# Feed-forward layers of a two-layer decoder trunk emitted as one planned stream

## The chip, the cores and the metric

One core of a Trainium2 chip runs the whole forward pass. The metric is the device time of one execution, in microseconds (us). The kernel before takes 2194.31 us, the median of three runs (2193.89 to 2194.33). Engines are named as in the profile: PE is TensorE's matmul, PEld its weight load, ACT is ScalarE, DVE is VectorE, POOL is GpSimd, SP is SyncE, which here only issues DMAs.

## The reference

The input x is 256 tokens by 2048 channels, float32. Each of two layers normalises, applies a mixer, adds the result to x, normalises again, applies the feed-forward part, and adds again. The mixer of layer 0 is a chunkwise matrix-memory recurrence beside a spatial-gating network, that of layer 1 is attention on keys chosen by an indexer. The change hardly touches the mixers. The feed-forward part is the same in both layers:

```
def conv_ffn(xn, w_up, conv_w, conv_b, w_down):      # 2048 -> 2*5632 -> 2048
    h = xn @ w_up
    h = depthwise_causal_conv(h, conv_w, width=3) + conv_b
    a, b = jnp.split(h, 2, axis=-1)
    return (jax.nn.silu(a) * b) @ w_down
```

All of it is wanted in float32 accuracy.

## The kernel before

**Matmuls in three passes.** Every operand is split into two halves that TensorE multiplies fast: hi, the value rounded to the type fp32r, and lo, what is left. A product is hi*hi + lo*hi + hi*lo: `mm3` (L175) issues three matmuls, L177, L178 and L179. The activations are the stationary operand, 128 tokens at a time, and the weights the moving one, 512 columns at a time. So a k-tile of 128 rows takes three matmuls for each of the two token halves.

**Loads and casts.** `load_w` (L88) brings one block of weights, four k-tiles by 512 columns, 1 MB, into a `raw` buffer with one DMA on SP (L93). Then it makes hi on ACT (a copy) and lo on DVE (raw minus hi), two k-tiles in one instruction; both are recorded under L65, the line of a helper. There are four `raw` buffers, four `hi` and four `lo` buffers, so hi and lo hold two blocks and raw four.

**Feed-forward.** `ffn` (L858) works in two parts, of 24 and of 20 tiles of 128 hidden channels. In a part it goes through the up-projection in groups of 512 columns, first four tiles of a, then the matching four of b, and so on; then it runs the down-projection of that part. A group is 16 k-tiles, four blocks, accumulated in two PSUM tiles `mm` (one per token half). The last block of a group is ordered so that the first token half ends first. There are 22 groups in a layer.

**What follows a group.** `up_job` (L819) is a Python generator that is resumed once per block by `pump` (L78). First it scales the PSUM tiles by the norm's factor on ACT (L823) and transposes 32x32 squares on DVE (L824) into `turn`. `LAG` blocks later 16 DMAs of 32 KB (L833) put the squares in place in a tile `A`, so that channels lie on partitions. Then the convolution runs for four tiles, two per resumption: ACT L840, DVE L842 and L844, and for the a half Silu on ACT (L847), for the b half the product with a (DVE L852) and the split into `yh` (ACT L184) and `yl` (DVE L185), which feed the down-projection.

**Order.** Code emits instructions in Python order, and a scheduler of the framework then orders each engine's queue, by the place of emission and by when buffers come free. Nothing fixes the order of casts against convolution on ACT and DVE. `resid` (L298) adds the down-projection to x in `h` and starts `norm_job` (L211), which transposes and splits the next layer's input; its end (L240 to L247) spreads the norm's factor over a row tile `rbc`, with four small matmuls in the profile (two instructions, L242). Only the mixer of layer 0 reads `rbc`, in `ch_sum`. `ch_proj` (L151), used twelve times in that mixer, has weights stationary and both activation halves side by side as the moving operand of 512 columns; a second matmul of 256 columns adds lo of the weights.

`out_steps(ktiles, row0, late)` (L316) lists the blocks of a down-projection. With `late` above zero the last `late` k-tiles of its first two column blocks come after the earlier ones of both.

## Time and profile before

| | |
|---|---|
| median of 3 runs | 2194.31 us |
| the profiled execution | 2193.54 us, span of the trace 2191.8 us |
| PE busy | 2168.8 us, 99% of the span |
| PEld busy | 1780.8 us, 81% |
| DVE busy | 1374.1 us, 63% |
| ACT busy | 1130.1 us, 52% |
| granted TensorE clock | 1.00 of full speed throughout |
| DMA | 425.51 MB, mean 194 GB/s |

The profile is one execution. The span runs from the first to the last instruction of the trace; the execution's own time is 1.7 us longer. Busy time is the time in which an engine has an instruction under way. Matmuls overlap one another, and their ends are modelled, so PE's busy share is not its speed. Each instruction has a start, a length, a line of the kernel, the tile it writes and those it reads, and, where the engine sat idle before it, what ended that wait.

### The profile page before, as it was taken

The page shows a single profiled execution, that of the slowest core. Times are in us where ns is not written, and L with a number is a line of the kernel's source. Part 1 is how long each engine was busy: PE and PEld are TensorE (multiplying, and loading weights), DVE is VectorE, ACT ScalarE, POOL GpSimd, SP SyncE. Part 2 cuts the span into 40 slices and gives each one's busy share as a digit, 9 for nine tenths or more (in the row PEclk, how much of TensorE's full clock was granted, in tenths as well). Part 3 has the DMA queues.
Part 4 walks back from the last instruction along what each step waited for, and adds up shares of the span by engine and source line. Part 5 has one row for each costly group of instructions (what it writes and reads, how often), then busy time and mean ns, then how long its engine had stood idle before and what let it go on. Part 6 is the DMA issues. An engine that isn't in the chain of part 4 may idle for free.

```text
span 2191.8 us, 27024 instructions
## 1 busy us (share of the span) xinstructions
PE 2168.8 (99%) x9948; PEld 1780.8 (81%) x9948; DVE 1374.1 (63%) x1903; ACT 1130.1 (52%) x1661; POOL 49.2 (2%) x69
## 2 busy tenths in 40 slices
PE   8999999999999999999999999999999999999999
PEld 7888888887778888777889888888777788877787
DVE  5455565575776446676656887556666754576664
ACT  6544555464555345555545566545555533554542
POOL 0011100000000000000000001000000000000000
PEclk9999999999999999999999999999999999999999
DMA  8555555667677556767656444456667655677673
GB/s 279 182 173 168 177 183 191 196 185 216 195 199 239 192 192 183 231 187 217 214 155 209 154 154 153 160 191 186 208 199 229 216 199 190 184 206 216 203 238 115
DMA packets 412033, 425.51 MB, mean 194 GB/s; under 512 B 198620, under 2 KB 236028, under 8 KB 411900
## 3 DMA queue, kind: packets, MB, share of 16 engines
q1 hardware_dynamic: 410476, 421.55, 62.0%
q10 hardware_dynamic: 1424, 2.23, 0.3%
q8 instruction: 78, 1.28, 0.3%
q14 instruction: 55, 0.45, 0.1%
HBM read 398.54 MB, written 2.10 MB: 183 GB/s over the span
## 4 chain that ended last, share of the span: by engine, by line
PE 78%; DVE 8%; issue 5%; ACT 4%; DMA 4%; POOL 0%; SPq 0%; ACTq 0%; DVEq 0%; POOLq 0%
PE mm L179 24%; PE mm L178 23%; PE mm L177 23%; PE mm L163 4%; DVE lo L65 3%; DMA raw<-in_ffn_w_up 3%; PE mm L161 2%; ACT hi L65 2%; ACT conv L840 2%; DVE conv L844 1%; DVE conv L842 1%; DVE turn L824 1%; DMA raw<-in_ffn_w_down 1%; PE tr L218 1%; DVE conv L852 1%
## 5 line engine op out<-in xcount | busy, mean ns | idle before, releaser
L65 DVE TENSOR_TENSOR lo<-raw,hi 128x1024 fp32r<-128x1024 f32 (+3 forms) x764 | 917.2, 1217 | 528.3 <-ACT hi L65 509.2
L65 ACT CAST hi<-raw 128x1024 fp32r<-128x1024 f32 (+3 forms) x764 | 779.0, 1037 | 629.3 <-PE mm L178 546.8
L177 PE MATMUL mm<-hi,xc 128*128 128x512 f32 (+3 forms) x1920 | 742.1, 387 | 9.3 <-ACT hi L65 8.7
L179 PE MATMUL mm<-lo,xc 128*128 128x512 f32 (+3 forms) x1920 | 737.8, 387 | 1.8
L178 PE MATMUL mm<-hi,xc 128*128 128x512 f32 (+3 forms) x1920 | 736.6, 384 | 0.0
L177 PEld LDWEIGHTS mm<-hi,xc 128*128 128x128 f32 x1920 | 360.9, 188 | 87.9 <-ACT hi L65 20.5
L179 PEld LDWEIGHTS mm<-lo,xc 128*128 128x128 f32 x1920 | 358.7, 188 | 85.4 <-DVE lo L65 19.4
L178 PEld LDWEIGHTS mm<-hi,xc 128*128 128x128 f32 x1920 | 361.1, 188 | 67.4
L177 PE MATMUL mm<-hi,yh 128*128 128x512 f32 x960 | 376.8, 394 | 1.7 <-ACT hi L65 1.6
L178 PE MATMUL mm<-hi,yl 128*128 128x512 f32 x960 | 375.8, 391 | 0.4 <-DVE yl L185 0.4
L179 PE MATMUL mm<-lo,yh 128*128 128x512 f32 x960 | 375.0, 392 | 0.3
L177 PEld LDWEIGHTS mm<-hi,yh 128*128 128x128 f32 x960 | 180.2, 188 | 42.1 <-ACT hi L65 3.3
L179 PEld LDWEIGHTS mm<-lo,yh 128*128 128x128 f32 x960 | 180.0, 188 | 41.5 <-DVE lo L65 2.9
L178 PEld LDWEIGHTS mm<-hi,yl 128*128 128x128 f32 x960 | 180.4, 188 | 39.2 <-DVE yl L185 1.2
L824 DVE STREAM_TRANSPOSE turn<-mm 128x512 f32<-128x512 f32 x88 | 62.8, 714 | 188.6 <-ACT mm L823 188.6
L823 ACT ACTIVATE mm<-mm,rstd 128x512 f32<-128x512 f32 x88 | 58.1, 660 | 210.7 <-PE mm L179 206.6
L163 PE MATMUL mm<-xc,hi 128*128 128x512 f32 x360 | 126.8, 395 | 0.0
L161 PE MATMUL mm<-xc,lo 128*128 128x256 f32 x384 | 106.2, 282 | 0.0
L840 ACT ACTIVATE conv<-A,conv 128x256 f32<-128x256 f32 x176 | 98.4, 594 | 1.3
L844 DVE SCALAR_TENSOR_TENSOR conv<-A,conv,conv 128x254 f32<-128x254 f32 x176 | 82.5, 480 | 3.5
L842 DVE SCALAR_TENSOR_TENSOR conv<-A,conv,conv 128x255 f32<-128x255 f32 x176 | 80.9, 472 | 4.8 <-ACT conv L840 4.8
L163 PEld LDWEIGHTS mm<-xc,hi 128*128 128x128 f32 x360 | 67.6, 188 | 15.1
(207 smaller groups left out, 861.0 us busy)
## 6 DMA issues: line engine op xcount, KB each, us to landing
raw<-in_ffn_w_up SPq DMA_DIRECT2D x176, 1024.0 KB
raw<-in_ffn_w_down SPq DMA_DIRECT2D x88, 1024.0 KB
raw<-in_even_w_in SPq DMA_DIRECT2D x44, 1024.0 KB
raw<-in_odd_w_in SPq DMA_DIRECT2D x24, 1024.0 KB
A<-turn SPq DMA_DIRECT2D x704, 32.0 KB
raw<-in_even_w_out SPq DMA_DIRECT2D x16, 1024.0 KB
raw<-in_odd_w_out SPq DMA_DIRECT2D x16, 1024.0 KB
raw<-in_odd_w_in SPq DMA_DIRECT2D x12, 736.0 KB
```

The lines of the kernel that those rows point to most:

```text
L65: ins = call(*args, **kw).ins
L161: nc.tensor.matmul(ps[ct][:, 1], wlo[:, c], x[:, 0], start=False, stop=False)
L163: nc.tensor.matmul(ps[ct], whi[:, c], x, start=False, stop=kt == KT - 1)
L177: nc.tensor.matmul(ps, ah, bh, start=start, stop=False)
L178: nc.tensor.matmul(ps, al, bh, start=False, stop=False)
L179: return nc.tensor.matmul(ps, ah, bl, start=False, stop=stop)
L218: nc.tensor.transpose(tp[:, tt * P:(tt + 1) * P], self.h[:, tt, kt * P:(kt + 1) * P], self.ident)
L823: nc.scalar.activation(ps[tt], ps[tt], AF.Copy, scale=self.rstd[:, tt:tt + 1])
L824: nc.vector.transpose(T[:, :, tt], ps[tt].rearrange("p (c t) -> p c t", c=4))
L840: nc.scalar.activation(y, A[:, ct], AF.Identity, bias=conv[:, 3, c:c + 1], scale=conv[:, 2, c:c + 1])
L842: nc.vector.scalar_tensor_tensor(y[:, 1:], A[:, ct, :S - 1], conv[:, 1, c:c + 1], y[:, 1:], op0=ALU.mult, op1=ALU.add)
L844: nc.vector.scalar_tensor_tensor(y[:, 2:], A[:, ct, :S - 2], conv[:, 0, c:c + 1], y[:, 2:], op0=ALU.mult, op1=ALU.add)
```

## The change

The two parts of a feed-forward layer, up and down, are put into one list of blocks, `plan`, and `stream` goes through it. At place i it emits the loads up to place i + 5 and the casts up to place i + 2, then the matmuls of place i; then it resumes the jobs and, at a group's end, starts the eviction. `flowed` chains every load, cast, eviction, transpose, turn DMA and convolution of the layer to the one emitted before it on the same engine, so that ACT, DVE and SP take them in the order of emission. `up_job` loses its lag and does one tile of convolution per block. The down-projection uses `late` = 4. `norm_job` stops after the norm's factor, except for the norm at the kernel's head. `ch_proj` issues hi for both column tiles, then lo for both, and lo is added to the other half of the PSUM tile. Buffers and their numbers stay as they are.

```diff
--- before.py
+++ after.py
@@ -31,7 +31,8 @@
 
 RAW = 2048
 HALF = 1024
-LAG = 3
+FETCH = 5
+CAST = 2
 
 NAMES = ["x", "mix_norm", "even_w_in", "even_i_bias", "even_f_bias", "even_a_norm",
          "even_b_norm", "even_spatial", "even_spatial_bias", "even_w_out", "odd_w_in",
@@ -145,6 +146,68 @@
                 evac(n, c0, ps)
                 del open_ps[n]
 
+    def flowed(self, eng, call, *args, **kw):
+        prev = self.flow.get(eng)
+        with self.tc.issue_after(prev) if prev is not None else nullcontext():
+            self.flow[eng] = call(*args, **kw).ins
+
+    def stream(self, plan):
+        nc = self.nc
+        raws, parts, open_ps, seen = [], [], {}, {}
+
+        def fetch(w, ktiles, step, lhs, evac, pre):
+            n, c0, ncol, k0, nk, row0 = step
+            raw = self.wraw.tile([P, RAW], F32, tag="raw", name="raw")
+            r0 = (row0 + k0) * P
+            self.flowed("p", nc.sync.dma_start, raw[:, :nk * ncol].rearrange("p (k c) -> p k c", k=nk),
+                        w[r0:r0 + nk * P, c0:c0 + ncol].rearrange("(k p) c -> p k c", p=P))
+            raws.append(raw)
+
+        def cast(w, ktiles, step, lhs, evac, pre):
+            n, c0, ncol, k0, nk, row0 = step
+            raw, per, got = raws[len(parts)], HALF // ncol, []
+            for s in range(0, nk, per):
+                m = min(per, nk - s)
+                hi = self.whi.tile([P, HALF], F32R, tag="hi", name="hi")
+                lo = self.wlo.tile([P, HALF], F32R, tag="lo", name="lo")
+                src, u = raw[:, s * ncol:(s + m) * ncol], m * ncol
+                self.flowed("s", nc.scalar.copy, hi[:, :u], src)
+                self.flowed("v", nc.vector.tensor_tensor, lo[:, :u], src, hi[:, :u], op=ALU.subtract)
+                got += [(k0 + s + i, hi[:, i * ncol:(i + 1) * ncol], lo[:, i * ncol:(i + 1) * ncol])
+                        for i in range(m)]
+            parts.append(got)
+
+        self.flow = {}
+        for i, (w, ktiles, step, lhs, evac, pre) in enumerate(plan):
+            if pre is not None:
+                pre()
+            n, c0, ncol, k0, nk, row0 = step
+            acts = [lhs(k0 + j) for j in range(nk)]
+            while len(raws) < min(i + 1 + FETCH, len(plan)):
+                fetch(*plan[len(raws)])
+            while len(parts) < min(i + 1 + CAST, len(plan)):
+                cast(*plan[len(parts)])
+            if n not in open_ps:
+                open_ps[n] = [self.mm.tile([P, 512], F32, tag="mm", name="mm") for _ in range(NT)]
+                seen[n] = 0
+            ps, work = open_ps[n], []
+            for (kt, whi, wlo), (ah, al) in zip(parts[i], acts):
+                work.append((ah, al, whi, wlo, seen[n] == 0, seen[n] == ktiles - 1))
+                seen[n] += 1
+            order = [(tt, j) for j in range(nk) for tt in range(NT)]
+            if seen[n] == ktiles:
+                order.sort()
+            for tt, j in order:
+                ah, al, whi, wlo, first, last = work[j]
+                t = slice(tt * P, (tt + 1) * P)
+                self.mm3(ps[tt][:, :ncol], ah[:, t], al[:, t], whi, wlo, first, last)
+            parts[i] = None
+            self.pump()
+            if seen[n] == ktiles:
+                evac(n, c0, ps)
+                del open_ps[n]
+        self.flow = None
+
     def tok_steps(self, n, c0, ncol, per=4, k0=0, k1=KT, row0=0):
         return [(n, c0, ncol, k, min(per, k1 - k), row0) for k in range(k0, k1, per)]
 
@@ -155,12 +218,10 @@
             for kt, whi, wlo in self.load_w(w, k0, 8, c0, 2 * P):
                 x = self.x_both(kt)
                 for ct in range(2):
-                    c = slice(ct * P, (ct + 1) * P)
-                    if kt == 0:
-                        nc.tensor.matmul(ps[ct], whi[:, c], x, start=True, stop=False)
-                    nc.tensor.matmul(ps[ct][:, 1], wlo[:, c], x[:, 0], start=False, stop=False)
-                    if kt > 0:
-                        nc.tensor.matmul(ps[ct], whi[:, c], x, start=False, stop=kt == KT - 1)
+                    nc.tensor.matmul(ps[ct], whi[:, ct * P:(ct + 1) * P], x, start=kt == 0, stop=False)
+                for ct in range(2):
+                    nc.tensor.matmul(ps[ct][:, 0], wlo[:, ct * P:(ct + 1) * P], x[:, 0],
+                                     start=False, stop=kt == KT - 1)
             self.pump()
         evac(ps)
 
@@ -235,6 +296,8 @@
         nc.vector.tensor_scalar(self.var, s, 1.0 / D, EPS, op0=ALU.mult, op1=ALU.add)
         self.rsqrt(self.rstd, self.var)
         self.ready.add("rstd")
+        if not head:
+            return
         yield 1
         yield 1
         tp = self.tr.tile([P, S], F32, tag="tr", name="tr")
@@ -820,40 +883,38 @@
         nc = self.nc
         T = fg.tile([P, 4, NT, P], F32, tag="turn", name="turn", bufs=2)
         for tt in range(NT):
-            nc.scalar.activation(ps[tt], ps[tt], AF.Copy, scale=self.rstd[:, tt:tt + 1])
-            nc.vector.transpose(T[:, :, tt], ps[tt].rearrange("p (c t) -> p c t", c=4))
-        yield 1
-        for _ in range(LAG):
-            yield 1
+            self.flowed("s", nc.scalar.activation, ps[tt], ps[tt], AF.Copy, scale=self.rstd[:, tt:tt + 1])
+            self.flowed("v", nc.vector.transpose, T[:, :, tt], ps[tt].rearrange("p (c t) -> p c t", c=4))
+        yield 1
         there = T.rearrange("p c t (q e) -> p q (c t) e", q=4)
         here = A.rearrange("p c (t i e) -> p i (c t) e", t=NT, i=4)
         for i in range(4):
             for q in range(4):
                 src, dst = slice(32 * i, 32 * i + 32), slice(32 * q, 32 * q + 32)
-                nc.sync.dma_start(here[dst, i], there[src, q])
+                self.flowed("p", nc.sync.dma_start, here[dst, i], there[src, q])
             if i % 2:
                 yield 1
         yield 1
         for ct in range(4):
             y = fg.tile([P, S], F32, tag="conv", name="conv")
             c = cc + ct
-            nc.scalar.activation(y, A[:, ct], AF.Identity, bias=conv[:, 3, c:c + 1],
-                                 scale=conv[:, 2, c:c + 1])
-            nc.vector.scalar_tensor_tensor(y[:, 1:], A[:, ct, :S - 1], conv[:, 1, c:c + 1], y[:, 1:],
-                                           op0=ALU.mult, op1=ALU.add)
-            nc.vector.scalar_tensor_tensor(y[:, 2:], A[:, ct, :S - 2], conv[:, 0, c:c + 1], y[:, 2:],
-                                           op0=ALU.mult, op1=ALU.add)
+            self.flowed("s", nc.scalar.activation, y, A[:, ct], AF.Identity, bias=conv[:, 3, c:c + 1],
+                        scale=conv[:, 2, c:c + 1])
+            for j in (1, 2):
+                self.flowed("v", nc.vector.scalar_tensor_tensor, y[:, j:], A[:, ct, :S - j],
+                            conv[:, 2 - j, c:c + 1], y[:, j:], op0=ALU.mult, op1=ALU.add)
             if sa is None:
-                nc.scalar.activation(A[:, ct], y, AF.Silu)
+                self.flowed("s", nc.scalar.activation, A[:, ct], y, AF.Silu)
                 self.ready.add(("a", c))
             else:
                 kt = kt0 + ct
                 assert ("a", c - 44) in self.ready
-                nc.vector.tensor_tensor(y, sa[:, ct], y, op=ALU.mult)
-                self.split(self.yh[kt // 4][:, kt % 4], self.yl[kt // 4][:, kt % 4], y)
+                self.flowed("v", nc.vector.tensor_tensor, y, sa[:, ct], y, op=ALU.mult)
+                hi, lo = self.yh[kt // 4][:, kt % 4], self.yl[kt // 4][:, kt % 4]
+                self.flowed("s", nc.scalar.copy, hi, y)
+                self.flowed("v", nc.vector.tensor_tensor, lo, y, hi, op=ALU.subtract)
                 self.ready.add(("y", kt))
-            if ct % 2:
-                yield 1
+            yield 1
 
     def ffn(self, l, gcol, final):
         nc, I, tc = self.nc, self.I, self.tc
@@ -862,30 +923,37 @@
         self.ready -= {("a", c) for c in range(44)}
         with tc.tile_pool(name=f"ff{l}", bufs=1) as ff, tc.tile_pool(name=f"fg{l}", bufs=2) as fg:
             As = [ff.tile([P, 4, S], F32, name=f"A{i}") for i in range(4)]
-
-            base = 0
+            plan, base = [], 0
             for part, nk in enumerate((24, 20)):
-                yh, yl = self.new_y(self.acts, 4)
-                eh, el = self.new_y(ff, (nk - 16) // 4, 4)
-                self.yh, self.yl = yh + eh, yl + el
+                last = part == 1
+
+                def open_y(nk=nk):
+                    yh, yl = self.new_y(self.acts, 4)
+                    eh, el = self.new_y(ff, (nk - 16) // 4, 4)
+                    self.yh, self.yl = yh + eh, yl + el
+
+                def up_evac(A, cc, sa, j):
+                    def evac(n, c0, ps):
+                        self.ensure("rstd")
+                        self.start(self.up_job(fg, ps, A, cc, conv, sa, j), now=True)
+                    return evac
+
+                pre = open_y
                 for j in range(0, nk, 4):
                     turn = (base + j) // 4 % 2
                     for half in range(2):
-                        A = As[2 * turn + half]
-                        sa = As[2 * turn] if half else None
-                        cc = 44 * half + base + j
-
-                        def evac(n, c0, ps):
-                            self.ensure("rstd")
-                            self.start(self.up_job(fg, ps, A, cc, conv, sa, j), now=True)
-
-                        self.tok_plan(w_up, self.x_at, KT, self.tok_steps(0, cc * P, 512), evac)
-                last = part == 1
-                if last and not final:
-                    self.new_xT()
-                self.tok_plan(w_down, self.y_at, nk, self.out_steps(nk, base, 0),
-                              self.resid(gcol if last else None, final=final and last))
+                        A, cc = As[2 * turn + half], 44 * half + base + j
+                        evac = up_evac(A, cc, As[2 * turn] if half else None, j)
+                        for step in self.tok_steps(0, cc * P, 512):
+                            plan.append((w_up, KT, step, self.x_at, evac, pre))
+                            pre = None
+                pre = self.new_xT if last and not final else None
+                evac = self.resid(gcol if last else None, final=final and last)
+                for step in self.out_steps(nk, base, 4):
+                    plan.append((w_down, nk, step, self.y_at, evac, pre))
+                    pre = None
                 base += nk
+            self.stream(plan)
 
     def run(self):
         self.new_xT()
```

On ACT, from the first eviction of the fifth group of layer 0 on, the order was (L823 is the eviction, L65 a cast, L840 the convolution's start, L184 makes yh):

```order
L823 ACTIVATE mm<-mm,rstd 128x512
L65 CAST hi<-raw 128x1024 x2
L823 ACTIVATE mm<-mm,rstd 128x512
L840 ACTIVATE conv<-A_3389,conv_101 128x256 x2
L184 CAST yh_3391<-conv 128x256 x2
L65 CAST hi<-raw 128x1024 x2
L840 ACTIVATE conv<-A_3389,conv_101 128x256 x2
L65 CAST hi<-raw 128x1024 x4
L184 CAST yh_3391<-conv 128x256 x2
```

and in the changed kernel (all under L152, the line in `flowed`), around the evictions of the third group:

```order
L152 CAST hi<-raw 128x1024 x2
L152 ACTIVATE conv<-A_3387,conv_101 128x256
L152 CAST yh_3390<-conv 128x256
L152 ACTIVATE mm<-mm,rstd 128x512 x2
L152 CAST hi<-raw 128x1024 x2
L152 ACTIVATE conv<-A_3387,conv_101 128x256
L152 CAST yh_3390<-conv 128x256
L152 CAST hi<-raw 128x1024 x2
L152 ACTIVATE conv<-A_3387,conv_101 128x256
L152 CAST yh_3390<-conv 128x256
```

Two tiles of convolution stood together between casts; now each pair of casts, one block's, is followed by one tile's convolution, and both evictions of a group stand together behind one of them.

On DVE, after the two transposes (L824) of the fourth group, all four tiles of a convolution (L842, L844) came before six casts:

```order
L824 STREAM_TRANSPOSE turn<-mm 128x4x128 x2
L842 SCALAR_TENSOR_TENSOR conv<-A_3388,conv_101,conv 128x255
L844 SCALAR_TENSOR_TENSOR conv<-A_3388,conv_101,conv 128x254
L842 SCALAR_TENSOR_TENSOR conv<-A_3388,conv_101,conv 128x255
L844 SCALAR_TENSOR_TENSOR conv<-A_3388,conv_101,conv 128x254
L842 SCALAR_TENSOR_TENSOR conv<-A_3388,conv_101,conv 128x255
L844 SCALAR_TENSOR_TENSOR conv<-A_3388,conv_101,conv 128x254
L842 SCALAR_TENSOR_TENSOR conv<-A_3388,conv_101,conv 128x255
L844 SCALAR_TENSOR_TENSOR conv<-A_3388,conv_101,conv 128x254
L65 TENSOR_TENSOR lo<-raw,hi 128x1024 x6
```

and in the changed kernel, around the transposes of the third group:

```order
L152 TENSOR_TENSOR lo<-raw,hi 128x1024 x2
L152 SCALAR_TENSOR_TENSOR conv<-A_3387,conv_101,conv 128x255
L152 SCALAR_TENSOR_TENSOR conv<-A_3387,conv_101,conv 128x254
L152 TENSOR_TENSOR conv<-A_3386,conv 128x256
L152 TENSOR_TENSOR yl_3394<-conv,yh_3390 128x256
L152 STREAM_TRANSPOSE turn<-mm 128x4x128 x2
L152 TENSOR_TENSOR lo<-raw,hi 128x1024 x2
L152 SCALAR_TENSOR_TENSOR conv<-A_3387,conv_101,conv 128x255
L152 SCALAR_TENSOR_TENSOR conv<-A_3387,conv_101,conv 128x254
L152 TENSOR_TENSOR conv<-A_3386,conv 128x256
```

Here too each block's two casts are followed by one tile's convolution, product and yl.

On PE, in `ch_proj` (L161 and L163 before), a k-tile's four matmuls alternated:

```order
L161 MATMUL mm<-xc_86,lo 128x256
L163 MATMUL mm<-xc_86,hi 128x512
L161 MATMUL mm<-xc_86,lo 128x256
L163 MATMUL mm<-xc_86,hi 128x512
L161 MATMUL mm<-xc_86,lo 128x256
```

and now stand in pairs (L221 and L223 in the changed kernel):

```order
L221 MATMUL mm<-xc_86,hi 128x512 x2
L223 MATMUL mm<-xc_86,lo 128x256 x2
L221 MATMUL mm<-xc_86,hi 128x512 x2
L223 MATMUL mm<-xc_86,lo 128x256 x2
```

The number of matmuls and of their columns is the same.

## Rows read from the trace of the kernel before

**Rows 1.** The page, first part: engine, busy us, share of the span, instructions.

```profile
PE 2168.8 (99%) x9948; PEld 1780.8 (81%) x9948; DVE 1374.1 (63%) x1903; ACT 1130.1 (52%) x1661; POOL 49.2 (2%) x69
```

**Rows 2.** Table by stretches: window, length, then each engine's busy us (instructions).

```profile
531.82:669.10 137.28, 134.69 (x578) 106.72 (x577) 93.32 (x133) 75.38 (x109) 0.00 (x0) 1.00 0.70 207
680.00:790.00 110.00, 110.00 (x482) 90.11 (x481) 58.33 (x63) 45.35 (x48) 0.00 (x0) 1.00 0.62 210
```

**Rows 3.** In order of time, PE, up stretch: start, length, engine, line [wait <- releaser].

```profile
562.51 0.39 PE L178 MATMUL mm<-hi,xc 128*128 128x512 f32 x1
...
563.19 0.39 PE L178 MATMUL mm<-hi,xc 128*128 128x512 f32 x1
...
577.79 0.39 PE L179 MATMUL mm<-lo,xc 128*128 128x512 f32 x1
578.58 0.50 PE L177 MATMUL mm<-hi,xc 128*128 128x512 f32 x1 [0.40 <-ACT hi L65]
...
579.83 0.73 PE L179 MATMUL mm<-lo,xc 128*128 128x512 f32 x2
580.41 0.39 PE L177 MATMUL mm<-hi,xc 128*128 128x512 f32 x1
```

**Rows 4.** Waits of PEld, whole run: waiter <- releaser: total us, times, longest.

```profile
PEld mm L177 <- ACT hi L65: 23.7, 32, 0.8
PEld mm L179 <- DVE lo L65: 22.4, 60, 0.5
```

**Rows 5.** In order of time, ACT, same stretch as the wait of rows 3.

```profile
572.68 0.66 ACT L823 ACTIVATE mm<-mm,rstd 128x512 f32<-128x512 f32 x1
...
575.59 0.42 ACT L847 ACTIVATE A<-conv 128x256 f32<-128x256 f32 x1 [1.24 <-DVE conv L844]
...
577.49 1.98 ACT L65 CAST hi<-raw 128x1024 fp32r<-128x1024 f32 x2
```

**Rows 6.** Groups by form, whole run: xcount | busy us, mean ns | idle before, releasers.

```profile
L65 DVE TENSOR_TENSOR lo<-raw,hi 128x1024 fp32r<-128x1024 f32 x730 | 887.0, 1232 | 497.6 <-ACT hi L65 482.2 <-DMA A<-turn 4.5 <-PE mm L178 3.6
L65 ACT CAST hi<-raw 128x1024 fp32r<-128x1024 f32 x730 | 752.6, 1049 | 604.0 <-PE mm L178 527.0 <-PE mm L163 42.4 <-issue 28.3
...
L844 DVE SCALAR_TENSOR_TENSOR conv<-A,conv,conv 128x254 f32<-128x254 f32 x176 | 82.5, 480 | 3.5
...
L852 DVE TENSOR_TENSOR conv<-A,conv 128x256 f32<-128x256 f32 x88 | 36.4, 421 | 0.7
```

**Rows 7.** In order of time, SP's queue, up stretch: start, time of issue.

```profile
551.77 5.17 SPq L833 DMA_DIRECT2D A<-turn  x8
...
557.63 6.93 SPq L833 DMA_DIRECT2D A<-turn  x8
```

**Rows 8.** The chain that ended last, in order of time: start, length, what.

```profile
519.03 9.12 DMA raw<-in_ffn_w_up
```

**Rows 9.** In order of time, PE, down-projection of 20 k-tiles in layer 0.

```profile
1047.93 0.39 PE L179 MATMUL mm<-lo,yh 128*128 128x512 f32 x1
...
1049.75 0.50 PE L178 MATMUL mm<-hi,yl 128*128 128x512 f32 x1 [0.18 <-DVE yl L185]
```

**Rows 10.** In order of time, PE, at the end of a norm in layer 0.

```profile
421.16 0.61 PE L242 MATMUL tr<-ident,rstd 128*128 128x128 f32 x4
421.52 0.48 PE L177 MATMUL mm<-hi,xc 128*128 128x512 f32 x1
421.84 0.39 PE L178 MATMUL mm<-hi,xc 128*128 128x512 f32 x1
```

**Rows 11.** In order of time, PE, in ch_proj of layer 0's mixer.

```profile
106.37 0.40 PE L161 MATMUL mm<-xc,lo 128*128 128x256 f32 x2
106.61 0.40 PE L163 MATMUL mm<-xc,hi 128*128 128x512 f32 x1
...
119.66 0.40 PE L163 MATMUL mm<-xc,hi 128*128 128x512 f32 x1
...
123.90 0.40 PE L163 MATMUL mm<-xc,hi 128*128 128x512 f32 x1
```

## The prediction

> **What bounds the kernel now.** I read the page's first part, then the table by stretches, then single stretches in order of time, and last the durations by group. Throughout, a "step" is one load of 1 MB (four k-tiles by 512 columns, 24 matmuls), a "group" the four steps of one up-projection tile, and "hi" and "lo" the halves into which ScalarE (ACT) and VectorE (DVE) split a load; making them is "casting".
>
> The page has TensorE busy for 2168.8 of 2191.8 us [rows 1], which seems to leave 23 us. But a matmul is recorded as 0.39 us long while undisturbed ones start closer: three of them between 562.51 and 563.19, so 0.227 us apart [rows 3]. A record goes on while nothing new starts; the measure is the distance between starts. Six groups of 96 matmuls took 137.28 us in an up stretch, 0.238 each; 110 us of a down stretch held 482 records, 0.228 each [rows 2]. At 0.227 a step is 5.45 us and a group 21.8.
>
> [...]
>
> Where the time goes: from 577.79 to 580.41 seven matmuls start (three in rows left out), in 2.62 us instead of 7 x 0.227 = 1.59, so 1.03 us are lost [rows 3]. The row at 578.58 names ACT's hi as what ended the wait. The wait table has 32 waits of a weight load for hi and 60 for lo [rows 4]: one and about two for each of 32 of the 44 up groups. ACT shows why: the second eviction of a group begins at 572.68, then ACT sits idle for 1.24 us until DVE's convolution lets Silu go at 575.59, and the casts for the group's second step begin at 577.49, 0.3 us before TensorE stops [rows 3, 5]. The casts lacked neither data nor room; they stood behind several tiles' convolution in the queue.
>
> **The change part by part.**
>
> 1. Feed-forward order. Casts come two steps ahead, one tile's convolution per step. With four hi and four lo buffers, two of each per step, the casts for step i+2 take the buffers of step i: the first may start in the middle of step i, the second at its end. I follow the worst place, a group's end E (step i is its last), in us after E, with the durations of rows 5 and 6 and ACT and DVE strictly in the new order. ACT: second hi to 1.05, convolution start to 1.65. DVE: lo to 2.3, two convolution steps of 0.48 to 3.25, product to 3.7. ACT: yh to 4.1 (taken as long as Silu, 0.42), the group's two evictions of 0.66 to 5.4, first hi of step i+3 to 6.45. DVE: its lo to 7.7. Step i+3 starts at 2 x 5.45 = 10.9, so 3.2 us are to spare; the second hi and lo end at 8.9 and are needed at 13.6.
>
> Does the chain keep up? A step with the product costs 0.42 (yh) + 1.05 (hi) + 2 x 1.23 (lo) + 2 x 0.48 + 0.42 (product) = 5.3 us; with Silu alone instead of yh and product 4.9. The two groups of a pair: 4 x 5.3 + 4 x 4.9 + 4 x 0.66 = 43.4 us, against 8 x 5.45 = 43.6 for the matmuls. These are full durations; rows independent of the one before start earlier (hi x2 takes 1.98, not 2.10 [rows 5]), so 43.4 leans high. It fits, closely.
>
> What is late next: loads. SyncE's queue has per group a load, eight turn DMAs into A, a load, eight more, two loads: the same cycle as before. The turn DMAs wait for both transposes of an eviction; taking these as long as the evictions (an estimate), they begin at about E + 6. Eight take 5.2 us, the load about 0.6, the next eight 6.9 [rows 7], so the two loads behind go out at E + 18.8. One load took 9.1 us to land in the chain [rows 8], and 1 MB at 207 GB/s [rows 2] is 5.1 us, so they land by 28 and 33; their first casts are due at 30 and 35.4. Two us are to spare, and 3.2 more before TensorE waits. The last turn DMA must land before the convolution begins at E + 22.9: issued by 18.8, with 4 us to go. If it is late, the convolution holds the casts behind it, and the same 3.2 us cover that.
>
> [...]
>
> So the loss of 32 x 1.03 = 33.0 us goes. Bounds: 33.0 if no group finds a new wait, 0 if each finds one as long, and below nothing if the chain sets the pace (rival C). I take all of it, since 3.2 us are to spare and the down stretch, with the same buffers and no convolution, runs at 0.228 [rows 2].
>
> 2. The down projection holds back the last four k-tiles of its first two column blocks (late = 4). Five matmuls, four of them in rows left out, took 1.82 us from 1047.93 to 1049.75 instead of 1.14, so 0.7 us are lost, and what ended the wait is DVE's yl [rows 9]. I count it once per layer, where the part has 20 k-tiles: its last y were read in the fifth step after the last eviction, now in the ninth. Gain 1.4; bounds 0 and 1.4. Four PSUM tiles are open at once, but the second pair opens four steps after the last eviction, which is long done.
>
> 3. norm_job stops after rstd, except in the first norm. From 421.16 to 421.84 start four L242 matmuls and one more whose follower is late, 0.68 us instead of 0.227, so 0.45 us each time [rows 10], three times: 1.35. The copy on ACT goes as well, hidden anyway. Bounds: 1.1 (three times the 0.36 from 421.16 to 421.52) and 1.4.
>
> 4. ch_proj, 12 calls of 16 k-tiles. Twelve lo-hi pairs took 4.24 us from 119.66 to 123.90, 0.353 each; two lo in a row took 0.24 [rows 11]. The new order hi, hi, lo, lo costs 2 x 0.23 + 0.24 = 0.70 against 0.707: 192 x 0.007 = 1.3 us gained. The sum of a hi after a hi is read from the feed-forward layers; 0.01 or 0.02 either way per four matmuls gives bounds of 3 gained and 4 lost.
>
> Sum: 2193.54 (the profiled execution: span 2191.8 and 1.7 around it) - 33.0 - 1.4 - 1.35 - 1.3 = 2156.5. The median of the runs, 2194.31, is 0.8 higher; so 2157.3.
>
> **The rivals.**
>
> A. Part of the loss comes back. For it: 43.4 against 43.6 is close, and loads have 2 us to spare. If each of the 32 groups keeps half its wait, 16.5 us: 2174. Against: the 3.2 us must be used up first, and a part of a layer has only five or six pairs of groups before a down stretch, in which ACT and DVE have little but casts.
>
> B. The waits don't come from the order but from loads or turn DMAs, and only move: parts 2 to 4 alone remain, 4 us: 2190. Against: the row at 578.58 names the cast, and a load is not among the three things that hi waited for longest [rows 6].
>
> C. Slower. In fixed order ACT and DVE are one chain, each waiting for the other several times a step. If each step costs 0.5 us more than counted (hand-overs between the engines, turn data late), a pair takes 47.4 us against 43.6: 22 pairs lose 3.8 each, 84 us, less 3.2 for each of the four parts, so 71 us against 33 regained: 2194 + 38 = 2232. It decides from about 45.7 us a pair, where the loss equals the 2 x 1.03 of before, that is 0.3 us more per step. For it: the fixed order cannot fill a gap with what is ready. Against: 43.4 leans high.
>
> **How the numbers follow.** The forecast has 0.70, with its own range of 2153 to 2163 (3 us more gained in part 4; 4 lost there and 2 us of waits left where a part starts). A has 0.17, spread over 2163 to 2185; B 0.06; C 0.07. What a measurement can tell from no change is 0.2%, 4.4 us. Faster: the forecast, A and a little of B, 0.88. Same: most of B, 0.05. Slower: C, 0.07. The range that leaves out two in ten is 2152 to 2172: the forecast and about half of A.
>
> **What would show it.** Right: starts 0.227 apart in an up stretch, a group in 21.8 us instead of 22.9; the waits of weight loads for hi and lo gone from the table; ACT's hi waiting for TensorE, never TensorE for hi; L242 four times, not sixteen. Part 1 is wrong if a weight load still waits for hi or lo once a group, or if ACT's convolution waits for a turn DMA and the cast behind it comes late; C shows as ACT and DVE alternating while TensorE waits. Part 2 is wrong if a matmul of a down stretch still waits for yl, part 4 if a hi after a hi starts more than 0.23 later.

## The result, and the profile after

The changed kernel takes 2157.22 us (median of 4 runs, 2156.84 to 2157.70), the kernel before beside it 2194.10 (2193.79 to 2194.33): a ratio of 0.983, interval 0.982 to 0.985. The forecast was 2157.3. The profiled execution took 2157.5 with a span of 2155.7, so 36.0 us less than the one of before.

First the page's busy line, which answers to [rows 1], and the first line of the chain that ended last:

```profile
PE 2145.4 (100%) x9936; PEld 1787.8 (83%) x9936; DVE 1396.1 (65%) x1903; ACT 1128.4 (52%) x1658; POOL 49.5 (2%) x69
...
PE 94%; issue 4%; DVE 1%; DMA 0%; POOL 0%; ACT 0%; SPq 0%; DVEq 0%; POOLq 0%
```

TensorE is now the whole chain. Its busy time fell by 23.4 us, the time by 36: busy time could not show what was to be had. The table by stretches of the changed kernel, for the first window of [rows 2]:

```profile
531.82:669.10 137.28, 137.28 (x607) 113.70 (x606) 101.86 (x139) 79.32 (x114) 0.00 (x0) 1.00 0.73 211
```

In the same 137.28 us stand 607 matmuls, one per 0.226 us, where there were 578. DVE and ACT are busier there because the same work is packed closer; the clock was full (1.00) both times. In order of time, the last step of one group and the first of the next (PE; it answers to [rows 3]):

```profile
546.32 0.39 PE L239 MATMUL mm<-hi,xc 128*128 128x512 f32 x1
546.54 0.39 PE L240 MATMUL mm<-lo,xc 128*128 128x512 f32 x1
546.77 0.39 PE L238 MATMUL mm<-hi,xc 128*128 128x512 f32 x1
```

The group's end (E = 546.77) can't be seen in the distances any more: 0.227 across it, no wait. Both rows of [rows 4] are gone from the wait table of the weight loads; the largest that is left on L238 is a single wait for xc:

```profile
PEld mm L238 <- ACT xc L66: 1.1, 1, 1.1
```

What waits now are ACT and DVE, as the first lines of ACT's wait table show:

```profile
ACT hi L152 <- PE mm L239: 304.2, 258, 3.2
ACT yh L152 <- DVE conv L152: 200.7, 88, 2.4
```

ACT's hi waits for TensorE to free a buffer, 258 times, and TensorE never for hi. (L152 is the helper that chains the instructions, so all of the stream has this line; the names tell them apart.) ACT across that group's end answers to [rows 5]:

```profile
546.74 1.06 ACT L152 CAST hi<-raw 128x1024 fp32r<-128x1024 f32 x1 [0.30 <-PE mm L239]
547.70 0.60 ACT L152 ACTIVATE conv<-A,conv 128x256 f32<-128x256 f32 x1
550.47 0.41 ACT L152 CAST yh<-conv 128x256 fp32r<-128x256 f32 x1 [2.17 <-DVE conv L152]
550.78 1.23 ACT L152 ACTIVATE mm<-mm,rstd 128x512 f32<-128x512 f32 x2
551.93 1.99 ACT L152 CAST hi<-raw 128x1024 fp32r<-128x1024 f32 x2
553.82 0.61 ACT L152 ACTIVATE conv<-A,conv 128x256 f32<-128x256 f32 x1
...
557.08 1.99 ACT L152 CAST hi<-raw 128x1024 fp32r<-128x1024 f32 x2
```

and DVE beside it:

```profile
550.00 0.43 DVE L152 TENSOR_TENSOR conv<-A,conv 128x256 f32<-128x256 f32 x1
...
553.00 2.36 DVE L152 TENSOR_TENSOR lo<-raw,hi 128x1024 fp32r<-128x1024 f32 x2 [0.22 <-ACT hi L152]
```

SyncE's queue, one group earlier (E = 525.01), answers to [rows 7]:

```profile
530.70 5.16 SPq L152 DMA_DIRECT2D A<-turn  x8
535.97 0.55 SPq L152 DMA_DIRECT2D raw<-in_ffn_w_up  x1
536.56 5.57 SPq L152 DMA_DIRECT2D A<-turn  x8
542.23 7.23 SPq L152 DMA_DIRECT2D raw<-in_ffn_w_up  x3
```

Where the 36 us came from, stretch by stretch (from the first matmul of a stretch to the next matmul behind it, the last one to its own last matmul; worked out from the matmuls' starts in the two traces, and in that of parts 2 to 4 alone, an experiment below):

```
                         before   parts 2-4   after     (us)
ch_proj                  149.76    149.30    149.30
up, 12 groups, layer 0   270.99    270.48    262.08
down, 24 k-tiles         133.24    133.24    132.07
up, 10 groups            223.84    223.80    217.60
down, 20 k-tiles         114.35    113.59    112.46
up, 12 groups, layer 1   271.01    270.52    262.08
down, 24 k-tiles         133.23    133.22    132.07
up, 10 groups            223.84    223.84    217.60
down, 20 k-tiles         111.29    110.46    109.31
```

The feed-forward layers give 36.5 us of it and ch_proj 0.5; against that the start of the program, up to ch_proj, is 0.9 us longer in this execution (106.69 against 105.80). That start lies between 105.24 and 107.38 us in the traces of all the kernels here, so it says nothing of the change. By the last two columns part 1 gives 8.4 + 6.2 + 8.4 + 6.2 = 29.3 us in the up stretches (before rounding) and about 1.15 in each of the four down stretches, 33.9 in all.

### The profile page after: what moved, and what is told of

It reads as the page before. It is cut to its first block, busy times and chain, and to the rows that moved or that the text cites. A ratio compares the mean times of both kernels' runs of the same rounds, so it can differ in the third digit from the quotient of the medians.

```text
span 2155.7 us, 27048 instructions
## 1 busy us (share of the span) xinstructions
PE 2145.4 (100%) x9936; PEld 1787.8 (83%) x9936; DVE 1396.1 (65%) x1903; ACT 1128.4 (52%) x1658; POOL 49.5 (2%) x69
## 4 chain that ended last, share of the span: by engine, by line
PE 94%; issue 4%; DVE 1%; DMA 0%; POOL 0%; ACT 0%; SPq 0%; DVEq 0%; POOLq 0%
PE mm L240 28%; PE mm L239 28%; PE mm L238 28%; PE mm L221 4%; PE mm L223 2%; PE tr L279 1%; PE sm L848 1%; DVE lo L66 0%; PE tr L867 0%; DMA raw<-in_even_w_in 0%; PE sm L550 0%; DVE acc L795 0%; DVE acc L804 0%; PE sm L622 0%; PE tr L840 0%
## 5 line engine op out<-in xcount | busy, mean ns | idle before, releaser
L152 DVE TENSOR_TENSOR lo<-raw,hi 128x1024 fp32r<-128x1024 f32 x528 | 638.4, 1224 | 400.9 <-ACT hi L152 362.1
L238 PE MATMUL mm<-hi,xc 128*128 128x512 f32 (+3 forms) x1920 | 738.3, 385 | 0.7 <-ACT xc L66 0.7
L152 ACT CAST hi<-raw 128x1024 fp32r<-128x1024 f32 x528 | 546.3, 1050 | 311.9 <-PE mm L239 304.2
L238 PEld LDWEIGHTS mm<-hi,xc 128*128 128x128 f32 x1920 | 361.1, 188 | 69.1 <-ACT xc L66 1.1
L66 DVE TENSOR_TENSOR lo<-raw,hi 128x1024 fp32r<-128x1024 f32 (+3 forms) x236 | 278.5, 1183 | 204.6 <-ACT hi L66 192.3
L238 PE MATMUL mm<-hi,yh 128*128 128x512 f32 x960 | 376.9, 393 | 0.0
L66 ACT CAST hi<-raw 128x1024 fp32r<-128x1024 f32 (+3 forms) x236 | 238.4, 1011 | 250.9 <-PE mm L239 162.1
L238 PEld LDWEIGHTS mm<-hi,yh 128*128 128x128 f32 x960 | 180.3, 188 | 38.1
L152 DVE SCALAR_TENSOR_TENSOR conv<-A,conv,conv 128x255 f32<-128x255 f32 x352 | 169.3, 481 | 6.3
L152 ACT CAST yh<-conv 128x256 fp32r<-128x256 f32 x88 | 35.7, 406 | 200.7 <-DVE conv L152 200.7
L221 PE MATMUL mm<-xc,hi 128*128 128x512 f32 x384 | 122.0, 399 | 0.0
L152 ACT ACTIVATE A<-conv 128x256 f32<-128x256 f32 x88 | 36.8, 418 | 157.0 <-DVE conv L152 157.0
L152 ACT ACTIVATE conv<-A,conv 128x256 f32<-128x256 f32 x176 | 105.3, 598 | 0.0
L223 PEld LDWEIGHTS mm<-xc,lo 128*128 128x128 f32 x384 | 72.1, 188 | 17.0
```

Of the source, the lines that this page charges most:

```text
L66: ins = call(*args, **kw).ins
L152: self.flow[eng] = call(*args, **kw).ins
L221: nc.tensor.matmul(ps[ct], whi[:, ct * P:(ct + 1) * P], x, start=kt == 0, stop=False)
L223: nc.tensor.matmul(ps[ct][:, 0], wlo[:, ct * P:(ct + 1) * P], x[:, 0], start=False, stop=kt == KT - 1)
L238: nc.tensor.matmul(ps, ah, bh, start=start, stop=False)
```

## The experiments

Three readings were left of why part 1 works. Q: only the casts' place counts, ahead of evictions and convolution in ACT's and DVE's queues. S: it is the spreading of the convolution, one tile per step. F: it is the fixed order of each engine. Loads five steps ahead and the one list of blocks come along with the casts in every kernel made from the changed one, and no run has the casts ahead without them; that loads are not what the casts lacked is read from the trace of the kernel before (in the part on the rivals). Each kernel ran once, with a profile, beside a run of the kernel before (2194.27 to 2195.19). Each edit is shown against the kernel named.

**Casts not ahead** (changed kernel).

```
-CAST = 2
+CAST = 0
```

> The changed kernel with casts no steps ahead (CAST = 0): loads, fixed order and one tile of convolution per step stay. Theory Q (place in the queue: the casts must stand ahead of the eviction that waits for TensorE): at a group's end ACT takes the two evictions (0.6 each) before the next step's first hi (1.05), so TensorE waits about 2.4 us for hi and 0.4 more for lo, 2.8 us in each of 44 groups: 2157 + 123 = 2280 us, between 2250 and 2300. Theory S (spreading the convolution is what counts) and theory F (the fixed order itself is what counts): 2157 to 2165, since both stay.

Measured: 2369.89. The direction is Q's, the size is 90 us beyond it. S and F fall as sufficient causes: order and spreading without the casts ahead are 175 us slower than the kernel before. The lag is gone from this kernel too, so the 175 us are not the price of the casts' place alone. In one up group ACT shows how:

```profile
572.33 0.60 ACT L152 ACTIVATE conv<-A,conv 128x256 f32<-128x256 f32 x1 [8.01 <-DMA A<-turn]
...
574.78 1.23 ACT L152 ACTIVATE mm<-mm,rstd 128x512 f32<-128x512 f32 x2
575.93 1.99 ACT L152 CAST hi<-raw 128x1024 fp32r<-128x1024 f32 x2
```

SyncE's queue there:

```profile
565.19 5.59 SPq L152 DMA_DIRECT2D A<-turn  x8
570.87 14.04 SPq L152 DMA_DIRECT2D raw<-in_ffn_w_up  x3
```

and PE:

```profile
573.26 0.39 PE L240 MATMUL mm<-lo,xc 128*128 128x512 f32 x1
577.03 0.50 PE L238 MATMUL mm<-hi,xc 128*128 128x512 f32 x1 [3.38 <-ACT hi L152]
...
578.29 0.80 PE L240 MATMUL mm<-lo,xc 128*128 128x512 f32 x1 [0.53 <-DVE lo L152]
578.88 0.63 PE L238 MATMUL mm<-hi,xc 128*128 128x512 f32 x1
...
581.44 0.40 PE L238 MATMUL mm<-hi,xc 128*128 128x512 f32 x1
```

The start of the convolution stands at the head of ACT's queue for 8.01 us, until the turn DMAs that SyncE issued by 570.78 have landed; the evictions and the next casts stand behind it, and TensorE runs dry. ACT's wait table has this wait 44 times, once per up group, and that of the weight loads has what TensorE waits for:

```profile
ACT conv L152 <- DMA A<-turn: 275.9, 44, 8.0
...
PEld mm L238 <- ACT hi L152: 133.9, 46, 4.9
PEld mm L240 <- DVE lo L152: 43.2, 48, 1.0
```

From 573.26 to 581.44 ten matmuls start, in 8.18 us instead of 10 x 0.227 = 2.27. Some 1.2 us of the 5.9 lost come after the wait: six distances of 0.43 instead of 0.227 (the last section).

**Casts one step ahead** (changed kernel).

```
-CAST = 2
+CAST = 1
```

> The changed kernel with casts one step ahead (CAST = 1). Theory Q: after the evictions the casts for the step after the next are done at about E + 3.6 (first lo) and are needed at E + 5.45, so 1.8 us are still to spare: 2157 us, at most 2160. A theory that the second step ahead is needed: a wait of a weight load for hi or lo once a group, 2165 to 2195 us.

Measured: 2156.32, and no wait for hi or lo of the feed-forward stream. The second step is not needed. But with one step the margin is mostly used: ACT's convolution stands at the head of the queue in wait of turn DMAs 38 times (52.2 us in all, at most 3.1), and no weight load waits for it; with two steps ahead it does so in no group. The time is 0.5 us below the lowest run of the changed kernel, which one run can't call a gain.

**No fixed order** (changed kernel; the scheduler orders each engine, casts ahead and spreading stay).

```
-        prev = self.flow.get(eng)
-        with self.tc.issue_after(prev) if prev is not None else nullcontext():
-            self.flow[eng] = call(*args, **kw).ins
+        call(*args, **kw)
```

> The changed kernel without the chaining: casts two steps ahead and one tile of convolution per step are emitted as before, but the scheduler orders ACT, DVE and SP. Theory F (fixed order is what counts): most of the loss returns, 2180 to 2195 us. Theories Q and S: most of the gain stays, 2157 to 2170 us.

Measured: 2157.85, with the up stretches at 262.07 and 217.60. The order on ACT did change: evictions now wait for TensorE 44 times (94.3 us in all), which they never do in the changed kernel. F falls.

**Casts ahead alone** (changed kernel without the fixed order, and with two tiles' convolution in every second step; the loads ahead, the missing lag and parts 2 to 4 stay):

```
-            yield 1
+            if ct % 2:
+                yield 1
+                yield 1
```

> Casts two steps ahead alone: no chaining, and two tiles of convolution every second step as before. Theory Q: the gain stays for the most part, 2157 to 2175 us. Theories S and F: the loss is back, 2185 to 2195 us.

Measured: 2157.21, stretches as in the changed kernel. S falls too: neither the fixed order nor the spreading is needed.

**Two tiles every second step, fixed order kept** (the edit above alone).

> The changed kernel with two tiles of convolution in every second step instead of one in each; casts ahead and fixed order stay. Theory Q: the second tile costs the chain of ACT and DVE about 2.3 us at a time and some 3.4 are to spare at the worst place, so 2157 to 2161 us. Theory S (spreading is what counts): a wait once a group, 2175 to 2195 us.

Measured: 2157.54.

**Spreading alone** (kernel before, one tile per step; the lag of three steps between evictions and turn DMAs goes as well, as it does in the change).

```
-LAG = 3
+LAG = 0
...
-            if ct % 2:
-                yield 1
+            yield 1
```

> The kernel before with its convolution spread in the code alone (one tile per step, no lag): casts where they were, no chaining. Theories Q and F: the scheduler can still put the casts behind an eviction and a convolution, 2185 to 2200 us. Theory S: 2157 to 2170 us.

Measured: 2255.0, which no theory had: 60 us slower than before. Two edits were in it, so the next run takes one away.

**The lag alone** (kernel before).

```
-LAG = 3
+LAG = 0
```

> The kernel before with its lag of three steps between evictions and turn DMAs set to 0, nothing else changed (two tiles' convolution every second step, casts not ahead). Theory L, the lag is what kept the convolution's start from standing in ACT's queue in wait of turn DMAs with casts behind it: about as slow as the kernel with one tile per step and no lag, 2235 to 2265 us, and ACT's conv waits for A<-turn in up groups. Rival R, spreading the convolution over every step did the harm there, the lag nothing: 2185 to 2200 us, no waits of conv for A<-turn.

Measured: 2252.78. (The bracket in the expectation is not exact: in the kernel before the two pairs of tiles stand in two consecutive steps.) So taking the lag away is the cause, and the spreading adds 2 us at most. ACT's wait table has the line that shows it:

```profile
ACT conv L840 <- DMA A<-turn: 91.5, 18, 7.8
```

and one of these waits in order of time:

```profile
572.36 1.10 ACT L840 ACTIVATE conv<-A,conv 128x256 f32<-128x256 f32 x2 [5.14 <-DMA A<-turn]
...
576.25 1.99 ACT L65 CAST hi<-raw 128x1024 fp32r<-128x1024 f32 x2 [0.17 <-DMA raw<-in_ffn_w_up]
```

It is the wait of the first experiment: in the kernel before, the lag of three steps gave the turn DMAs time to land before the convolution came to the head of ACT's queue. Without it the convolution stands there in 18 of the 44 up groups, casts behind it, and the up stretches are 14 to 19 us longer. The down stretches are shorter, though: 132.0 and, with 20 k-tiles, 112.4 and 109.3 us, which is what they take in the changed kernel. In the kernel before, the lag carries the last group's convolution further into them.

Why the changed kernel, without lag as well, doesn't have this wait can be read from its rows. With casts ahead the convolution stands behind casts that must wait for TensorE to free their buffers, and so it comes up late by itself: its first row, 547.70, is 22.7 us after the end of its group (525.01), when the last turn DMA had been issued 5.6 us before (536.56 + 5.57). Without casts ahead it was at the head at 564.32 (572.33 - 8.01), with 6.5 us of turn DMAs still to be issued. The delay put in by hand is replaced by one that follows TensorE.

**Casts ahead alone, the lag kept** (the kernel with casts ahead alone, plus the lag).

```
+LAG = 3
...
         yield 1
+        for _ in range(LAG):
+            yield 1
```

> Casts two steps ahead alone, with the lag of three steps kept: two tiles' convolution every second step, no fixed order between jobs and stream. Theory Q, only the place of the casts ahead of evictions and convolution counts: 2157 to 2165 us (the upper end, if the last y of a part now come three steps later and the down-projection waits for them). Rival: the gain needs the lag gone as well, because convolution three steps later meets the next group's evictions: 2170 to 2195 us, with waits of weight loads for hi or lo once a group.

Measured: 2172.24, between the two. Q's number was missed, and the number lies in the rival's range; but the rival's sign, weight loads that wait for hi or lo, is absent, and Q's mechanism holds: the up stretches are 262.08 and 217.60, the same as after to the last digit. All that is lost stands in the two down stretches with 20 k-tiles (119.75 and 116.93 against 112.46 and 109.31, 14.9 us). The weight loads' wait table has the line for it, and PE in order of time one of the four:

```profile
PEld mm L237 <- ACT yh L151: 10.6, 4, 4.7
```

```profile
1053.14 0.80 PE L237 MATMUL mm<-hi,yh 128*128 128x512 f32 x1 [4.25 <-ACT yh L151]
```

The last y of the part come too late for the ninth step of the down-projection. So in up stretches neither lag, spreading nor order counts once the casts lead, and taking the lag away serves the last y of a part.

**Parts 2 to 4 alone** (kernel before; the changed ch_proj is in the diff of the change):

```
+        if not head:
+            return
...
-self.out_steps(nk, base, 0)
+self.out_steps(nk, base, 4)
```

> The kernel before with the three small parts alone: late = 4, norm_job cut short, ch_proj reordered. The prediction's prices, 1.4 + 1.35 + 1.3 = 4 us: 2190 us; with what the changed kernel's ch_proj shows (0.5 us) 2191. If they help the feed-forward order indirectly: below 2185 us.

Measured: 2189.5, so 4.8 us for what the prediction put at 4.05. By the table of stretches: 0.8 in each down stretch with 20 k-tiles, 0.5 at each L242 of an up stretch and 0.4 in the second mixer, 0.46 in ch_proj; that makes 3.5. The rest is what differs between executions: the start of the program is 0.6 us shorter here than in the profiled kernel before, and the kernel before ran 0.8 us longer beside this run (2194.34) than when it was profiled (2193.54).

**Without the held-back k-tiles** (changed kernel).

```
-                for step in self.out_steps(nk, base, 4):
+                for step in self.out_steps(nk, base, 0):
```

> The changed kernel with late = 0 in the down projection. The convolution of the last group ends in the seventh step after its eviction, but its y are read in the fifth (20 k-tiles) or sixth (24), so three and two tiles are made at once: about 3.5 us of waiting for the one and 2 for the other, per layer: 2157 + 11 = 2168 us. If late = 4 is worth only the 1.4 us priced in the prediction: 2158.6 us.

Measured: 2163.87, so they are worth 6.6 us there, against 1.4 and against the 11 expected here. All four down stretches are longer, by 1.0, 1.9, 1.0 and 1.95. TensorE in the second of them:

```profile
1037.45 0.74 PE L238 MATMUL mm<-hi,yh 128*128 128x512 f32 x2 [0.31 <-ACT yh L152]
1039.89 0.74 PE L238 MATMUL mm<-hi,yh 128*128 128x512 f32 x2 [0.77 <-ACT yh L152]
```

and ACT:

```profile
1037.00 0.40 ACT L152 CAST yh<-conv 128x256 fp32r<-128x256 f32 x1 [1.53 <-DVE conv L152]
1037.31 0.60 ACT L152 ACTIVATE conv<-A,conv 128x256 f32<-128x256 f32 x1
1039.44 0.40 ACT L152 CAST yh<-conv 128x256 fp32r<-128x256 f32 x1 [1.53 <-DVE conv L152]
```

Read in the fifth step, the last y are made on demand, one tile behind the other, each through ACT and DVE in turn (2.44 us from yh to yh). With the same `late` = 0, the kernel before without its lag has down stretches as short as those of the changed kernel (above): there the convolution does not stand behind casts that wait for TensorE. So the casts ahead make the last y late, and the k-tiles held back give that time back.

**Loads four and three steps ahead** (changed kernel, FETCH = 4, and FETCH = 3).

> The changed kernel with loads four steps ahead instead of five. By the prediction's account of the loads (two us to spare behind the turn DMAs, and over 3 us of casts in hand) the load behind the second eight turn DMAs goes out 17 us after a group's end, lands by 26 and is due at 24.5: 1.5 us late, which the casts in hand cover: 2157 to 2160 us. If the depth of the loads carries the gain: a wait once a group, 2175 us or more.

Measured: 2157.38. The fifth step is not needed.

> The changed kernel with loads three steps ahead. The load between the two sets of turn DMAs goes out 11.4 us after a group's end, lands by 18.5 to 20 and is due at 13.6: 5 to 6.5 us late, with 3.4 in hand, so TensorE waits 1.5 to 3 us in each group: 2220 to 2290 us, slower than the kernel before. If loads have much more to spare than counted: 2157 to 2165 us.

Measured: 2252.42. ACT's wait table has a line that no other kernel here has in this size, with what the weight loads then wait for; below it stands an up group on ACT:

```profile
ACT hi L152 <- DMA raw<-in_ffn_w_up: 125.6, 69, 4.1
...
PEld mm L240 <- DVE lo L152: 77.7, 107, 1.0
PEld mm L238 <- ACT hi L152: 40.1, 83, 1.8
```

```profile
580.58 2.00 ACT L152 CAST hi<-raw 128x1024 fp32r<-128x1024 f32 x2 [2.91 <-DMA raw<-in_ffn_w_up]
582.48 0.60 ACT L152 ACTIVATE conv<-A,conv 128x256 f32<-128x256 f32 x1
```

With three steps the casts ahead wait for their loads, and the convolution behind them is late with them. One step less than needed costs 95 us, one more than needed brings nothing.

## Why the prediction was right

**What bounds the kernel.** Right: by distances between starts 36 us were lost (33.0 + 1.4 + 1.35, the terms of parts 1 to 3), where the busy time of [rows 1] left 23, and 36.0 came back. One sentence of the reading is not exact: a record does not go on until something new starts (that at 577.79 ends at 578.18, the next begins at 578.58 [rows 3]); being 0.39 us long, it hides at most 0.16 us of a distance. A group takes 21.76 us (groups start at 525.01 and 546.77), foretold as 21.8.

**Part 1.** 33.0 foretold, 33.9 came (the table of stretches): 29.3 in the up stretches and 4.6 where down stretches begin. The 32 waits were counted rightly but placed wrongly. Of the weight loads' waits for hi, the kernel before has 8 in an up stretch of 12 groups (first line, 393 to 664 us) and one at the start of the down stretch behind it (second line, 664 to 800 us):

```profile
PEld mm L177 <- ACT hi L65: 5.9, 8, 0.8
...
PEld mm L177 <- ACT hi L65: 0.8, 1, 0.8
```

Over the whole run 28 stand in up groups and 4 at the starts of down stretches, where the convolution of the last group is still to be done; the window of [rows 2] from 680 us on, which the prediction took for a down stretch without loss, begins behind that wait. 28 x 1.03 and 4 x 1.03 are 28.8 and 4.1, near the 29.3 and 4.6 measured. No group found a new wait. The chain at a group's end went as worked out. With E = 546.77, foretold and then read from the rows above:

```
                                foretold   read    from
second hi done                   E+1.05    1.03    546.74 + 1.06
product done                       3.7     3.66    550.00 + 0.43
evictions done                     5.4     5.24    550.78 + 1.23
second lo of step i+3 done         8.9     8.6     553.00 + 2.36
turn DMAs begin (E = 525.01)       6       5.7     530.70
loads behind them go out          18.8    17.2     542.23
step with the product              5.3     5.15    551.93 to 557.08
```

The first lo of step i+3 was done 3.4 us before its step (by the matmuls' starts), foretold 3.2; 43.4 us a pair did lean high. In the run without casts ahead, the casts at 575.93 had their buffers free from about 568.0 on (when the group's last 24 matmuls began, 573.26 - 23 x 0.227) and started only behind the convolution, which waited for a DMA until 572.33, and what follows it. In the 8.01 us of that wait ACT started nothing else.

What the prediction left undivided is which edit does it. It followed casts, spreading and order as one; the runs show that with the casts one step ahead all of it comes in the up stretches, that spreading and fixed order give nothing that can be measured, and that the lag's removal, which it did not price, is worth 15 us once casts are ahead (it spares the last y) and costs 58 where they are not.

**Part 2.** 1.4 foretold; 1.6 measured alone in the old order (0.8 in each down stretch with 20 k-tiles), but 6.6 when undone in the changed kernel. The term was right as a gain over the kernel before; the part does more in the new order, which part 1's own sum had taken for granted: the casts ahead make the y of the last group late, and they must have time.

**Part 3.** 1.35 foretold. In the kernel with parts 2 to 4 alone 0.5 + 0.4 + 0.5 came, 1.4; L242's four matmuls between 421.16 and 421.52 [rows 10] are gone from the stretch, and matmuls follow each other at 0.227 there. The two instructions of L242, 128 columns of float32 each, took 0.36 us, 0.18 each; a matmul of the fp32r halves takes 0.227 for 512 columns [rows 3].

**Part 4.** 1.3 foretold, 0.46 came (149.76 to 149.30). In ch_proj, PE in order of time:

```profile
119.68 0.40 PE L223 MATMUL mm<-xc,lo 128*128 128x256 f32 x2
119.91 0.63 PE L221 MATMUL mm<-xc,hi 128*128 128x512 f32 x2
...
123.86 0.40 PE L223 MATMUL mm<-xc,lo 128*128 128x256 f32 x2
```

Six cycles in 4.18 us, 0.697 each, are even a little better than the 0.70 foretold. The term was mis-sized by what it was compared with: the 0.707 of [rows 11] is from one call and does not stand for all twelve. By the medians of each call's matmul starts, four matmuls took 0.701 to 0.712 us before in seven calls but 0.693 to 0.694 in the other five; after, 0.697 to 0.698 in all twelve. So seven calls gain and five lose a little.

**The sum.** Parts 1 to 4 give 33.9 + 1.6 + 1.4 + 0.5 = 37.4 us, foretold 37.05; 36.0 of it show in the profiled execution, whose start is 0.9 us longer; the other 0.5 was not followed. That the forecast of 2157.3 meets the median of 2157.22 within 0.1 us is luck: single parts were off by up to 0.9 us, upward and downward, and the start alone differs by more from one execution to the next.

**The rivals.** A (part of the loss comes back): no group kept a wait. B (loads or turn DMAs are the cause): in the kernel before, ACT's casts wait for a load only three times in the whole run, 4.5 us, all in the first mixer's weights and none in the feed-forward layers; so the loads were not the cause. They stay narrow, as three steps ahead show, but four are enough. C (the chain of ACT and DVE sets the pace): not in the changed kernel, where a step takes 5.15 of 5.45 us. Its other half, a convolution that waits for turn DMAs with casts behind it, is what the kernels with neither casts ahead nor lag do, at 2253 to 2370.

## What to carry to other kernels

Where one queue holds the work that feeds the bottleneck and work that waits for slow partners, give the first its place at least one step ahead of the second (the convolution waited up to 8.01 us for DMAs here, with the casts behind it); here the order and spacing of the rest then hardly mattered. A delay put in by hand (the lag) may be what keeps such a wait from the head of a queue: see what comes there before it is removed. Measure what the bottleneck still has to give by the distances between its starts, not by its busy time (36 us against 23 here), and undo each edit by itself: here one edit of several made nearly all of the gain.

## What the runs showed of the hardware

The mean granted clock of TensorE was below 1.000 in four runs. The kernel without casts ahead has 0.976 (a weight load waits up to 4.9 us for hi), the kernel before with its lag removed 0.982 and 0.983 (two runs, up to 3.7 and 3.9 us), casts ahead with the lag kept 0.997 (two waits of 4.25 us, one per layer; 0.61 in the stretch from 1053.14 to 1060.00 behind the first), the others 1.000. The table by stretches of the kernel without casts ahead, around the pause shown above (window, length, busy us of PE, PEld, DVE, ACT and POOL, granted clock, DMA share, GB/s):

```profile
560.00:573.30 13.30, 13.30 (x61) 10.97 (x59) 4.57 (x6) 2.98 (x5) 0.00 (x0) 1.00 0.67 155
573.30:578.29 4.99, 1.09 (x5) 0.30 (x3) 4.09 (x8) 3.82 (x6) 0.00 (x0) 0.97 0.44 169
578.29:584.00 5.71, 5.71 (x19) 4.60 (x20) 4.65 (x7) 2.93 (x5) 0.00 (x0) 0.73 0.56 184
584.00:590.00 6.00, 6.00 (x28) 4.99 (x27) 4.93 (x8) 2.81 (x4) 0.00 (x0) 1.00 0.80 205
```

After a wait of 3.38 us and one of 0.53 the clock is 0.73 in the mean of the next 5.7 us: matmuls of 512 columns start 0.43 us apart from 578.88 to 581.44 and 0.227 apart again after that. So this pause costs 1.2 us more than its own length (six distances, 0.2 us more each). The waits of up to 0.8 us in the kernel before cost nothing of the kind (clock 1.00 in [rows 2]), nor did the weight loads' waits of up to 1.8 us in the kernel with loads three steps ahead (1.000 over the whole run). Two waits of one length differed in what followed: in the kernel without casts ahead TensorE sits idle for 1.7 us until 418.47 and again until 870.03, and the clock is 1.00 in the mean after the first (until 424) and 0.71 after the second (until 876). What decides it was not shown. The lower clock is one reason why that kernel was further off than expected. The larger one is the wait for turn DMAs in every group, which the expectation did not have: weight loads waited 177 us (133.9 + 43.2) where 123 were expected, and an estimate of the clock's part is what is left of the 213 us lost, 36.
